# Hybrid encoder block: first weights in tiles of their own, the second unit's product ahead of the norm sum, and buffers placed at equal bytes modulo 512

## The chip, the cores and the metric

The kernel runs on one core of one Trainium2 chip. The metric is the device time of one execution in microseconds (us). Lower is better. A core has a matrix engine (PE; its weight loads are listed apart as PEld), a vector engine (DVE), a scalar engine (ACT), a general engine (POOL) and a queue engine (SP) that issues most transfers. Matrix products read two operands from the on-chip memory SBUF (a stationary one, loaded first, and a moving one, streamed past it) and write to PSUM, which has eight banks here, each holding one tile of 128x512 floats.

## The reference

One residual block over 512 frames of 1024 features:

```python
x = x + 0.5 * swiglu(rms_norm(x, ffn1_norm), ffn1_w1, ffn1_w3, ffn1_w2)   # D_FF = 2816
h = rms_norm(x, mix_norm); p = h @ w_in
y_a = rwkv7(token_shift(p_rwkv)) @ rwkv_proj      # 8 heads, delta-rule state
y_b = forgetting_attention(p_fox) @ fox_proj      # 8 heads
x = x + (sigmoid(g_a) * y_a + sigmoid(g_b) * y_b) @ w_out
x = x + 0.5 * swiglu(rms_norm(x, ffn2_norm), ffn2_w1, ffn2_w3, ffn2_w2)
out = rms_norm(x, final_norm)

def rms_norm(x, g): return x * rsqrt(mean(x * x) + 1e-6) * g
def swiglu(h, w1, w3, w2): return (silu(h @ w1) * (h @ w3)) @ w2
```

## The kernel before, in words

The activations are kept transposed: `xT` is eight tiles of 128 features by 512 frames. Every float operand of a large product is split into a high part in a reduced float format and a low part, the remainder (`xh`/`xl` for the scaled input, `whi`/`wlo` for weights, `hh`/`hl` for the hidden layer). `mm3` (line 124) makes each product out of three: high by high, high by low, low by high. One product of 128x128 weights with a 128x512 tile is one matmul instruction, so eight 128-feature slices give 24 instructions for one tile of output.

**Weights.** `load_raw` (line 105) brings 128x1024 floats (512 KB) into one of three `raw` buffers through SP's queue. `split_w` (line 111) casts them to `whi` on ACT and subtracts to `wlo` on DVE (on POOL where told so). There are two `whi` and two `wlo` buffers.

**The first FFN.** A unit `j` of the 22 hidden tiles takes two output tiles, `pa` (w1) and `pb` (w3), 24 instructions each. They are evacuated with the factor `rstd` of the norm: `fa = pa * rstd`, `fs = silu(fa)`, `fb = pb * rstd`, `fh = fb * fs`, and then split to `hh`, `hl`. The norm's factor is applied behind the product, so that the products need only `xT` times the gain. The first unit's products (named `f` in the trace) are run while the input is still arriving and being transposed (`xtp`, line 231). Then `Norm.finish` (line 189) adds up the squares, splits the sum, forms the sum over all features with two matmuls by a matrix of ones (`ssum`), and takes the root (`rln`, `rstd`) on ACT. After the 22 units come the down products `pd` (line 345): eight output tiles of 66 instructions, moving operand `hh` or `hl`. The second FFN is the same with other weights, its last output tile cut into two halves of 256 frames.

**The middle.** The mixer's input product (tiles `pk`, `pgt`, `pq`, `pv`), the chunked delta rule, attention, two projections (`ppj`, moving operands `yh`/`yl` and `ya`) and the output product (`pw`, moving operands `mh`/`ml`).

**PSUM.** Three pools: `pm` with two banks, `pr` with three, `pf` with three. `f0`, `f1`, every `pa`, `pd`, `pw`, `ppj` and `pgt` take a bank of `pm`; `pb`, `xtp` and `ssum` take one of `pr`.

**Order.** The code is recorded once. A scheduler then fixes each engine's order from its own estimate of times, within what the code allows; at run time each engine takes its instructions strictly in that order, each waiting for its own inputs and for its output buffer.

**Places in SBUF.** Tiles are laid one behind the other by pool in 32-byte steps. The following places are bytes within a partition, modulo 512, as the tile sizes give them; weights slices are 512 bytes apart and frame tiles 2048, so all slices of one buffer have the same remainder.

| buffers | before | changed |
|---|---|---|
| `raw`, `whi`, `wlo`, `xh`, `xl`, `acc`, `rstd`, temporaries | 288 | 288 |
| `hh`, `hl` (hidden layer of both FFNs), `xin` | 416 | 288 |
| mixer pool `sp`: `G`, `BK`, `RD`, `Tall`, and in their place later `ya`, `mh`, `ga` | 320 | 288 |
| `V4` (later `ml1`) | 320 | 288 |
| `qk`, `kb`, `klc`, `tr`, `vt`, and later `yh`, `yl` | 480 | 288 |
| most work tiles of the mixer's preparation (`t2`) | 416 | 224 |
| `xT` | 480 | 480 |
| `ident`; `center`, `bonesr`, `onesr` | 128; 384 | 128; 384 |

Of the kernel before, what the change touches and what calls it, by code (L numbers as in the profile page):

```python
# [36 lines left out]
PAR_Q, PAR_K, PAR_F = 66, 67, 68  # L37
PAR_N = 69

COL_W = 3 * DA  # L40
# [10 lines left out]
def kernel(  # L51
# [51 lines left out]

    def load_raw(aps, kt, n):
        raw = wp.tile([P, kt, n], F32, tag="raw", name="raw", bufs=3)
        for c0, src in aps:
            nc.sync.dma_start(raw[:, :, c0:c0 + src.shape[1]],
                              src.rearrange("(k p) c -> p k c", p=P))
        return raw

    def split_w(raw, kt, n, eng=None, own=None):
        if own is None:
            hi = wp.tile([P, kt, n], F32R, tag="whi", name="whi", bufs=2)
            lo = wp.tile([P, kt, n], F32R, tag="wlo", name="wlo", bufs=2)
        else:
            hi, lo = [xp.tile([P, kt, n], F32R, tag=f"x{i}{own}", name=f"own{i}{own}") for i in "hl"]
        act.copy(hi[:], raw[:])  # L117
        (eng or dve).tensor_tensor(lo[:], raw[:], hi[:].bitcast(F32), op=ALU.subtract)  # L118
        return hi, lo
# [14 lines left out]

    def exact(ps, mat, src):
        hi, lo = tmp("shi", dt=F32R), tmp("slo", dt=F32R)
        act.copy(hi[:], src)
        dve.tensor_tensor(lo[:], src, hi[:].bitcast(F32), op=ALU.subtract)
        pe.matmul(ps, mat[:], hi[:], start=True, stop=False)
        pe.matmul(ps, mat[:], lo[:], start=False, stop=True)  # L140

# [10 lines left out]
    class Norm:  # L152
# [35 lines left out]

        def finish(s):
            ps = bank("ssum", pr)  # L190
            dve.tensor_tensor(s.acc[:], s.acc[:], s.last[:], op=ALU.add)
# [4 lines left out]
            act.activation(s.rstd[:], ln[:], AF.Exp, scale=-0.5)  # L196

        def cols(s, ps, whi, wlo, m, holes=()):
# [15 lines left out]
    for _ in range(8):  # L214
        pe.matmul(warm[:, 0:P], ones[:], ones[:], start=True, stop=True)
    gtp = bank("gtp", pr)
# [3 lines left out]
    with tc.tile_pool(name="x0", bufs=1) as x0:  # L220
        xin = [x0.tile([P, NB, D // 4], F32, name=f"xin{g}") for g in range(4)]
        first = []
        for g in range(4):
            nc.sync.dma_start(xin[g][:], x[0, :, g * 256:(g + 1) * 256].rearrange("(b p) c -> p b c", p=P))
            for w, at in ((ffn1_w1, 0), (ffn1_w3, 1)):
                if g == at:
                    first.append(load_raw([(0, w[0][:, 0:P])], KD, P))
        for c in range(KD):
            ps = bank("xtp", pr)
            for b in range(NB):  # L230
                pe.transpose(ps[:, b * P:(b + 1) * P], xin[c // 2][:, b, (c % 2) * P:(c % 2 + 1) * P], ident[:])
            cx = act.copy(xT[c][:], ps[:])
            nrm.scale(c, act if (85 >> c) & 1 else dve)
            for i, at in enumerate((0, 2)):
                if c == at:
                    first[i] = (bank(f"f{i}"), split_w(first[i], KD, P, (dve, pool)[i]))
# [71 lines left out]
    def ffn(nrm, w1, w3, w2, nxt, during=(), first=None, final=None):  # L308
        with tc.tile_pool(name="hp", bufs=1) as hp:
            hh, hl = [], []  # L310
            for j in range(KF):
                c0 = j * P
                if j == 0 and first:
# [11 lines left out]
                a = tmp("fa")  # L325
                dve.tensor_tensor(a[:], pa[:], nrm.rstd[:], op=ALU.mult)  # L326
                sa = tmp("fs")
                act.activation(sa[:], a[:], AF.Silu)
                b = tmp("fb")
                dve.tensor_tensor(b[:], pb[:], nrm.rstd[:], op=ALU.mult)  # L330
                h = tmp("fh")
                dve.tensor_tensor(h[:], b[:], sa[:], op=ALU.mult)
                hi = hp.tile([P, T], F32R, name=f"hh{j}")
                lo = hp.tile([P, T], F32R, name=f"hl{j}")
                split(hi[:], lo[:], h[:], "dve")
                hh.append(hi)
                hl.append(lo)
            cuts = ((0, 8), (8, 8), (16, 6))
# [40 lines left out]
    with ExitStack() as mx:  # L379
# [21 lines left out]
        dve.tensor_scalar(omu[:], par[:, PAR_MU:PAR_W0], -1.0, 1.0, op0=ALU.mult, op1=ALU.add)  # L401

        def shifted(o, src, rows, mu):
# [58 lines left out]

        PC = rp.tile([P, NP, NC], F32, name="PC")
        Ld = dp.tile([P, C, C], F32, name="Ld")
# [222 lines left out]
        for b in range(NB):  # L687
            o = vtp.tile([P, T], F32, name=f"vt{b}", tag=f"vt{b}")
            act.activation(o[:], vps[b][:], AF.Copy, scale=rc[:, b:b + 1])
# [98 lines left out]
        for p in range(NP):  # L788
# [5 lines left out]
            for q in range(2):  # L794
# [229 lines left out]
```

## Time and profile before

| what | value |
|---|---|
| median of three runs | 1213.7 us (1209.55 to 1213.95) |
| span of the profiled execution | 1210.2 us |
| the profiled execution's own time beside the span | not listed on the page; the median run is 3.5 us above the span |
| PE busy | 1184.5 us, 98% of the span |
| DVE, ACT, POOL busy | 55%, 38%, 8% |
| transfers | 122.54 MB, mean 101 GB/s |

The page gives busy time by engine; busy matmul time includes overlap of one matmul with the next, so the distance from start to start tells more than the duration of one. A row of the timeline reads: start in us, duration in us, engine, line, operation, output<-inputs, and in brackets how long the engine had been idle and what released it. A row of the windows view gives, for one stretch of time, each engine's busy time with the number of instructions, then the granted clock of PE (1.00 is full), the transfers' share and GB/s.

### The profile page before, as it was taken

To read this page: it belongs to the slowest core of one execution; us is meant where nothing else is said; L and a number is where in the kernel's file an instruction comes from. 1 tells how busy PE (TensorE), PEld (TensorE's weight loads), DVE (VectorE), ACT (ScalarE), POOL (GpSimd) and SP (SyncE) were. 2 spreads that over 40 slices of the span, in tenths; PEclk is the share of its full clock that TensorE was granted. 3 is DMA by queue.
4 is the path that set the end of the run, shared out by engine and by line. 5 is a ranking of instruction groups with operands and counts; after the bars stand their busy time and mean duration, and the time that the engine had idled before them with its cause. 6 is when DMAs were issued, how large, how long until landed. Compare 5 with 4: busy or idle time off the path is not lost.

```text
span 1210.2 us, 15874 instructions
## 1 busy us (share of the span) xinstructions
PE 1184.5 (98%) x6334; PEld 955.1 (79%) x6334; DVE 665.2 (55%) x993; ACT 458.1 (38%) x739; POOL 100.5 (8%) x144
## 2 busy tenths in 40 slices
PE   8999999999999999999999999999999999999997
PEld 6788888888887788887667777678888888888887
DVE  7454555443443688776766666865554445443232
ACT  5222222222222854445867655523322222222221
POOL 4100000001111111321000011111000000000110
PEclk9999999999999999999999999999999999999999
DMA  6233233333334234345113235532333333323331
GB/s 186 73 95 105 87 105 88 104 95 108 107 111 106 76 104 124 109 135 131 36 36 102 63 97 163 178 106 87 103 102 92 100 104 88 104 80 96 96 96 70
DMA packets 208152, 122.54 MB, mean 101 GB/s; under 512 B 9902, under 2 KB 200430, under 8 KB 208078
## 3 DMA queue, kind: packets, MB, share of 16 engines
q1 hardware_dynamic: 202078, 108.67, 31.1%
q0 software_dynamic: 3760, 12.06, 3.2%
q8 instruction: 50, 0.82, 0.3%
q10 hardware_dynamic: 2240, 0.79, 0.3%
q14 instruction: 24, 0.20, 0.1%
HBM read 110.82 MB, written 10.68 MB: 100 GB/s over the span
## 4 chain that ended last, share of the span: by engine, by line
PE 93%; DVE 3%; ACT 1%; issue 0%; DMA 0%; DVEq 0%; POOL 0%; POOLq 0%
PE pd L127 7%; PE pd L125 7%; PE pd L126 7%; PE pa L125 7%; PE pa L126 7%; PE pa L127 6%; PE pb L127 6%; PE pb L126 6%; PE pb L125 6%; PE pgt L125 3%; PE pgt L127 2%; PE pgt L126 2%; PE pk L125 2%; PE pk L127 2%; PE pk L126 2%; PE pw L127 1%
## 5 line engine op out<-in xcount | busy, mean ns | idle before, releaser
L117 ACT CAST whi<-raw 128x1024 fp32r<-128x1024 f32 (+3 forms) x199 | 198.2, 998 | 631.2 <-PE pa L126 180.7
L118 DVE TENSOR_TENSOR wlo<-raw,whi 128x1024 fp32r<-128x1024 f32 (+2 forms) x198 | 229.5, 1159 | 142.3 <-ACT whi L117 142.2
L125 PE MATMUL pa<-xh,whi 128*128 128x512 f32 x344 | 134.7, 392 | 2.6 <-DVE fa L326 2.6
L127 PE MATMUL pb<-xh,wlo 128*128 128x512 f32 x344 | 134.5, 391 | 0.9 <-DVE wlo L118 0.9
L126 PE MATMUL pa<-xl,whi 128*128 128x512 f32 x344 | 134.6, 391 | 0.0
L125 PE MATMUL pb<-xh,whi 128*128 128x512 f32 x344 | 134.5, 391 | 0.0
L126 PE MATMUL pb<-xl,whi 128*128 128x512 f32 x344 | 134.5, 391 | 0.0
L127 PE MATMUL pa<-xh,wlo 128*128 128x512 f32 x344 | 134.4, 391 | 0.0
L127 PE MATMUL pd<-hh,wlo 128*128 128x512 f32 x330 | 130.8, 396 | 0.0
L125 PE MATMUL pd<-hh,whi 128*128 128x512 f32 x330 | 130.3, 395 | 0.0
L126 PE MATMUL pd<-hl,whi 128*128 128x512 f32 x330 | 130.3, 395 | 0.0
L330 DVE TENSOR_TENSOR fb<-pb,rstd 128x512 f32<-128x512 f32 x43 | 29.7, 691 | 137.5 <-PE pb L127 137.5
L125 PEld LDWEIGHTS pa<-xh,whi 128*128 128x128 f32 x344 | 64.9, 189 | 16.7 <-DVE fa L326 3.1
L127 PEld LDWEIGHTS pb<-xh,wlo 128*128 128x128 f32 x344 | 65.0, 189 | 14.8 <-DVE wlo L118 1.3
L127 PEld LDWEIGHTS pa<-xh,wlo 128*128 128x128 f32 x344 | 65.0, 189 | 13.6
L126 PEld LDWEIGHTS pa<-xl,whi 128*128 128x128 f32 x344 | 65.0, 189 | 13.5
L126 PEld LDWEIGHTS pb<-xl,whi 128*128 128x128 f32 x344 | 65.0, 189 | 13.5
L125 PEld LDWEIGHTS pb<-xh,whi 128*128 128x128 f32 x344 | 64.9, 189 | 13.5
L126 PEld LDWEIGHTS pd<-hl,whi 128*128 128x128 f32 x330 | 62.0, 188 | 14.9
L125 PEld LDWEIGHTS pd<-hh,whi 128*128 128x128 f32 x330 | 62.0, 188 | 14.6
L127 PEld LDWEIGHTS pd<-hh,wlo 128*128 128x128 f32 x330 | 62.0, 188 | 14.6
L326 DVE TENSOR_TENSOR fa<-pa,rstd 128x512 f32<-128x512 f32 x43 | 29.7, 692 | 73.6 <-PE pa L127 73.6
(395 smaller groups left out, 1968.0 us busy)
## 6 DMA issues: line engine op xcount, KB each, us to landing
raw<-in_ffn_w_dram SPq DMA_DIRECT2D x118, 512.0 KB
raw<-in_w_in_dram SPq DMA_DIRECT2D x40, 512.0 KB
raw<-in_ffn_w_dram SPq DMA_DIRECT2D x15, 384.0 KB
raw<-in_w_out_dram SPq DMA_DIRECT2D x8, 512.0 KB
gsave<-gs SPq DMA_DIRECT2D x9, 256.0 KB
xin<-in_x_dram SPq DMA_DIRECT2D x4, 512.0 KB
xsave<-xT POOLq DMA_DIRECT2D x8, 256.0 KB, 2.3
G<-gsave POOLq DMA_DIRECT2D x8, 256.0 KB, 3.8
```

The lines of the kernel that those rows point to most:

```text
L117: act.copy(hi[:], raw[:])
L118: (eng or dve).tensor_tensor(lo[:], raw[:], hi[:].bitcast(F32), op=ALU.subtract)
L125: pe.matmul(ps, whi, xhi, start=first, stop=False)
L126: pe.matmul(ps, whi, xlo, start=False, stop=False)
L127: return pe.matmul(ps, wlo, xhi, start=False, stop=last)
L326: dve.tensor_tensor(a[:], pa[:], nrm.rstd[:], op=ALU.mult)
L330: dve.tensor_tensor(b[:], pb[:], nrm.rstd[:], op=ALU.mult)
```

## The change

In words:

- The first unit's weights get raw tiles and split tiles of their own, in the pool `x0` that holds the input while it arrives (`wraw`, `first`). The three `raw`, two `whi` and two `wlo` buffers are then free for the second unit from the start.
- The second unit's `pa` takes a bank of the pool `pf`, where it took one of `pm`.
- `Norm.finish` is cut into `gather` (last addition and split), `sums` (the two matmuls) and `root` (logarithm and exponential). In the first FFN `gather` stands ahead of the second unit, and `sums` is to be issued only after the last matmul of the second unit's `pa`. The evacuation of a unit waits in a list until `rstd` is there.
- The matrix `ones` loses its own buffer (a temporary for the start, then the same bits read out of `onesr`); `tiny` and the `mx` tiles are widened to 32 floats, `PC` and the `vt` tiles are allocated earlier, and 48 floats are added behind `vt`. This moves the buffers as in the table above.

No arithmetic instruction is added or taken away.

```diff
-    ones = cp.tile([P, P], F32, name="ones")
-    dve.memset(ones[:], 1.0)
+    ones_ = tmp("ones", (P, P))
+    dve.memset(ones_[:], 1.0)
     onesr = cp.tile([P, P], F32R, name="onesr")
-    dve.tensor_copy(onesr[:], ones[:])
+    dve.tensor_copy(onesr[:], ones_[:])
+    ones = onesr[:].bitcast(F32)
...
+        elif isinstance(own, int):
+            hi, lo = [xp.tile([P, kt, n], F32R, tag=f"x{i}{own}", name=f"own{i}{own}") for i in "hl"]
         else:
-            hi, lo = [xp.tile([P, kt, n], F32R, tag=f"x{i}{own}", name=f"own{i}{own}") for i in "hl"]
+            hi, lo = own
...
-    def exact(ps, mat, src):
+    def halved(src):
         hi, lo = tmp("shi", dt=F32R), tmp("slo", dt=F32R)
         act.copy(hi[:], src)
         dve.tensor_tensor(lo[:], src, hi[:].bitcast(F32), op=ALU.subtract)
-        pe.matmul(ps, mat[:], hi[:], start=True, stop=False)
-        pe.matmul(ps, mat[:], lo[:], start=False, stop=True)
+        return hi, lo
+
+    def summed(ps, mat, parts):
+        for i, part in enumerate(parts):
+            pe.matmul(ps, mat[:], part[:], start=i == 0, stop=i == 1)
...
-        def finish(s):
-            ps = bank("ssum", pr)
+        def gather(s):
             dve.tensor_tensor(s.acc[:], s.acc[:], s.last[:], op=ALU.add)
-            exact(ps[:], onesr, s.acc[:])
+            s.parts = halved(s.acc[:])
+
+        def sums(s):
+            s.ps = bank("ssum", pr)
+            summed(s.ps[:], onesr, s.parts)
+
+        def root(s):
             ln = tmp("rln")
-            ln_act(ln[:], ps[:], bias=epsr[:, 0:1], scale=1.0 / D)
+            ln_act(ln[:], s.ps[:], bias=epsr[:, 0:1], scale=1.0 / D)
...
         xin = [x0.tile([P, NB, D // 4], F32, name=f"xin{g}") for g in range(4)]
+        own = [[x0.tile([P, KD, P], F32R, name=f"first{i}{w}") for i in "hl"] for w in range(2)]
+        wraw = [x0.tile([P, KD, P], F32, name=f"wraw{w}") for w in range(2)]
...
-                    pa = bank("pa")
+                    pa = bank("pa", pf if early else pm)
                     pb = bank("pb", pr)
                     for ps, w in ((pa, w1), (pb, w3)):
-                        nrm.cols(ps[:], *load_w([(0, w[0][:, c0:c0 + P])], KD, P), P)
+                        mms = nrm.cols(ps[:], *load_w([(0, w[0][:, c0:c0 + P])], KD, P), P)
+                        if early and w is w1:
+                            with tc.issue_after(mms[-1].ins):
+                                nrm.sums()
+                            nrm.root()
+                            evacuate()
                 if j == 0:
-                    nrm.finish()
+                    nrm.gather()
+                    if not first:
+                        nrm.sums()
+                        nrm.root()
...
-        tiny = rp.tile([P, 2], F32, name="tiny")
+        tiny = rp.tile([P, PAD], F32, name="tiny")
...
+        vts = [vtp.tile([P, T], F32, name=f"vt{b}", tag=f"vt{b}") for b in range(NB)]
+        vtp.tile([P, 48], F32, name="vtpad", tag="vtpad")
...
-            mx_ = [tp.tile([P, 2 * NB], F32, tag=f"mx{q}", name=f"mx{q}", bufs=2) for q in range(2)]
+            mx_ = [tp.tile([P, PAD], F32, tag=f"mx{q}", name=f"mx{q}", bufs=2) for q in range(2)]
```

How the instructions move is seen at three places. The first is PE's order at the end of the first unit's products (`f`). Before, the sum over features follows at once:

```order
L127 MATMUL f0_156<-xh7_274,wlo_158 128x512
L125 MATMUL f1_187<-xh7_274,whi_188 128x512
L126 MATMUL f1_187<-xl7_275,whi_188 128x512
L127 MATMUL f1_187<-xh7_274,wlo_189 128x512
L139 MATMUL ssum_317<-shi_319,onesr_87 128x512
L125 MATMUL pb_343<-xh0_152,whi_376 128x512
```

Now the second unit's `pa` follows:

```order
L132 MATMUL f1_189<-xh7_274,firstl1_141 128x512
L130 MATMUL pa_322<-xh0_156,whi_326 128x512
L131 MATMUL pa_322<-xl0_157,whi_326 128x512
L132 MATMUL pa_322<-xh0_156,wlo_327 128x512
L130 MATMUL pa_322<-xh1_172,whi_326 128x512
L131 MATMUL pa_322<-xl1_173,whi_326 128x512
```

All 24 matmuls of that `pa` stand ahead of the first `ssum`; the second `ssum` stands behind eleven of `pb`'s 24 matmuls, where it stood behind 23.

The second place is ACT's order around the squares (`sq`) and the second unit's weight casts (`whi`). Before:

```order
L178 ACTIVATE sq_295<-xT4_112 128x512
L178 ACTIVATE sq_298<-xT5_113 128x512
L178 ACTIVATE sq_301<-xT6_114 128x512
L178 ACTIVATE sq_304<-xT7_115 128x512
L117 CAST whi_346<-raw_344 128x1024
L117 CAST whi_376<-raw_374 128x1024
L137 CAST shi_319<-acc_284 128x512
L130 ACT_TABLE_LOAD
```

Now both casts and the table load stand among the squares; DVE's subtractions (`wlo`) stand likewise between its additions of the squares:

```order
L189 ACTIVATE sq_295<-xT4_112 128x512
L122 CAST whi_326<-raw_324 128x1024
L135 ACT_TABLE_LOAD
L122 CAST whi_376<-raw_374 128x1024
L189 ACTIVATE sq_298<-xT5_113 128x512
L189 ACTIVATE sq_301<-xT6_114 128x512
L189 ACTIVATE sq_304<-xT7_115 128x512
L142 CAST shi_318<-acc_284 128x512
```

The third place is SP's queue behind the input. Before, the loads of the second unit (`raw_344`, `raw_374`) and of the third (`raw_418`) stand apart, with small parameter rows between them:

```order
L224 DMA xin3_137<-in_x_dram 128x4x256
L107 DMA raw_344<-in_ffn1_w1_dram 128x8x128
L277 DMA rows_308<-in_mix_norm_dram 8x128
L277 DMA rows_308<-in_ffn2_norm_dram 8x128
L277 DMA rows_308<-in_shift_mu_dram 12x128
```

Now the three loads follow the input directly and the rows come behind them:

```order
L247 DMA xin3_137<-in_x_dram 128x4x256
L110 DMA raw_324<-in_ffn1_w1_dram 128x8x128
L110 DMA raw_374<-in_ffn1_w3_dram 128x8x128
L110 DMA raw_418<-in_ffn1_w1_dram 128x8x128
L300 DMA rows_308<-in_mix_norm_dram 8x128
```

Behind the third unit, every engine's order is as before.

More of the change, by code (lines that the diff above doesn't have):

```diff
@@ L101, with load_raw @@
     sel = cp.tile([P, 8], F32, name="sel")
-    def load_raw(aps, kt, n):
-        raw = wp.tile([P, kt, n], F32, tag="raw", name="raw", bufs=3)
+    def load_raw(aps, kt, n, raw=None):
+        if raw is None:
+            raw = wp.tile([P, kt, n], F32, tag="raw", name="raw", bufs=3)
         for c0, src in aps:
@@ L214 @@
     for _ in range(8):
-        pe.matmul(warm[:, 0:P], ones[:], ones[:], start=True, stop=True)
+        pe.matmul(warm[:, 0:P], ones_[:], ones_[:], start=True, stop=True)
     gtp = bank("gtp", pr)
@@ L235 @@
                 if c == at:
-                    first[i] = (bank(f"f{i}"), split_w(first[i], KD, P, (dve, pool)[i]))
+                    first[i] = (bank(f"f{i}"), split_w(first[i], KD, P, (dve, pool)[i], own[i]))
             for i, at in enumerate((0, 2)):
@@ L309, in ffn, with evacuate @@
         with tc.tile_pool(name="hp", bufs=1) as hp:
-            hh, hl = [], []
+            hh, hl, done = [], [], []
+            def evacuate():
+                while done:
+                    j, pa, pb = done.pop(0)
+                    a = tmp("fa")
+                    dve.tensor_tensor(a[:], pa[:], nrm.rstd[:], op=ALU.mult)
+                    sa = tmp("fs")
+                    act.activation(sa[:], a[:], AF.Silu)
+                    b = tmp("fb")
+                    dve.tensor_tensor(b[:], pb[:], nrm.rstd[:], op=ALU.mult)
+                    h = tmp("fh")
+                    dve.tensor_tensor(h[:], b[:], sa[:], op=ALU.mult)
+                    hi = hp.tile([P, T], F32R, name=f"hh{j}")
+                    lo = hp.tile([P, T], F32R, name=f"hl{j}")
+                    split(hi[:], lo[:], h[:], "dve")
+                    hh.append(hi)
+                    hl.append(lo)
             for j in range(KF):
                 c0 = j * P
+                early = j == 1 and first
                 if j == 0 and first:
@@ L324, in ffn @@
                         during[j]()
[L325 to L337, printed above, removed]
+                done.append((j, pa, pb))
+                if nrm.rstd is not None:
+                    evacuate()
             cuts = ((0, 8), (8, 8), (16, 6))
```

13 lines of the change are left out of this document (10 added, 3 removed).

## The prediction

> **What bounds the kernel now.** I read the page first, then the chain, then the start in windows and instruction by instruction.
>
> ```profile
> span 1210.2 us, 15874 instructions
> PE 1184.5 (98%) x6334; PEld 955.1 (79%) x6334; DVE 665.2 (55%) x993; ACT 458.1 (38%) x739; POOL 100.5 (8%) x144
> PE 93%; DVE 3%; ACT 1%; issue 0%; DMA 0%; DVEq 0%; POOL 0%; POOLq 0%
> ```
>
> PE is busy 98% of the span and holds 93% of the chain that ends last; transfers hold none of it. So time can only come from two things: places where PE stands still or runs at a lower clock, and the distance from one matmul's start to the next. The windows of the start show the first (PE, PEld, DVE, ACT, POOL busy, then the granted clock):
>
> ```profile
> core 0: us, PE busy (x) PEld busy (x) DVE busy (x) ACT busy (x) POOL busy (x), PEclk, DMA share, GB/s
> 24.41:27.82 3.41, 1.29 (x4) 0.79 (x5) 3.41 (x3) 2.43 (x3) 3.32 (x3) 1.00 0.13 37
> 27.82:31.24 3.42, 3.42 (x10) 2.65 (x8) 0.63 (x1) 0.00 (x0) 2.94 (x15) 0.50 0.87 257
> 34.65:38.06 3.41, 0.81 (x4) 0.68 (x5) 2.52 (x3) 3.35 (x5) 0.00 (x0) 1.00 0.05 16
> 38.06:41.48 3.42, 3.42 (x10) 2.68 (x9) 1.81 (x3) 0.35 (x1) 0.00 (x0) 0.50 0.47 138
> ```
>
> Twice PE works only 1.29 and 0.81 us of 3.41, and each time the next 3.4 us run at a clock of 0.50. The timeline names the waits:
>
> ```profile
> 23.53 0.39 PE L127 MATMUL f<-xh,wlo 128*128 128x512 f32 x1
> 25.61 0.50 PE L139 MATMUL ssum<-shi,onesr 128*128 128x512 f32 x1 [1.70 <-ACT shi L137]
> 27.49 0.53 PE L127 MATMUL pb<-xh,wlo 128*128 128x512 f32 x1 [0.91 <-DVE wlo L118]
> 34.21 0.40 PE L127 MATMUL pb<-xh,wlo 128*128 128x512 f32 x1
> 37.25 0.50 PE L125 MATMUL pa<-xh,whi 128*128 128x512 f32 x1 [2.64 <-DVE fa L326]
> 49.87 0.39 PE L125 MATMUL pb<-xh,whi 128*128 128x512 f32 x1
> ```
>
> PE waits for the norm sum's operand, then for the second unit's `wlo`, and after `pb` for `fa`, which empties the bank of `pm` that `pa` needs. The engines behind these waits:
>
> ```profile
> 17.56 1.15 ACT L178 ACTIVATE sq<-xT 128x512 f32<-128x512 f32 x2
> 18.01 2.32 DVE L168 SCALAR_TENSOR_TENSOR xl<-xT,par,xh 128x512 fp32r<-128x512 f32 x2
> 23.05 1.99 ACT L117 CAST whi<-raw 128x1024 fp32r<-128x1024 f32 x2 [1.38 <-PE f L126]
> 23.43 0.91 DVE L191 TENSOR_TENSOR acc<-acc,sq 128x512 f32<-128x512 f32 x1
> 24.26 3.17 DVE L118 TENSOR_TENSOR wlo<-raw,whi 128x1024 fp32r<-128x1024 f32 x2
> 25.58 1.28 ACT L130 ACT_TABLE_LOAD   x1
> 35.13 0.68 ACT L132 ACTIVATE rln<-ssum,epsr 128x512 f32<-128x512 f32 x1
> 35.84 0.63 ACT L196 ACTIVATE rstd<-rln 128x512 f32<-128x512 f32 x1
> 36.50 0.69 DVE L326 TENSOR_TENSOR fa<-f,rstd 128x512 f32<-128x512 f32 x1
> ```
>
> The casts at 23.05 were released by PE: the second unit's weights had to wait until the first unit gave up its `whi` buffers.
>
> The second thing shows in PE's starts, in the up products, the down products and a projection, and for `pw` in a window of matmuls alone:
>
> ```profile
> 130.11 0.39 PE L125 MATMUL pb<-xh,whi 128*128 128x512 f32 x1
> ...
> 131.47 0.39 PE L125 MATMUL pa<-xh,whi 128*128 128x512 f32 x1
> ```
>
> ```profile
> 299.97 0.40 PE L125 MATMUL pd<-hh,whi 128*128 128x512 f32 x1
> ...
> 302.30 0.40 PE L126 MATMUL pd<-hl,whi 128*128 128x512 f32 x1
> ```
>
> ```profile
> 780.63 0.40 PE L125 MATMUL ppj<-ya,whi 128*128 128x512 f32 x1
> ...
> 782.97 0.40 PE L126 MATMUL ppj<-ya,whi 128*128 128x512 f32 x1
> ```
>
> ```profile
> 804.00:834.00 30.00, 30.00 (x130) 1.00 0.37 108
> ```
>
> Up: 6 steps in 1.36 us, 226.7 ns. Down: 10 steps in 2.33 us, 233 ns. `ppj`: 10 steps in 2.34 us, 234 ns. `pw`: 130 in 30 us, less one cut at the edges, 233 ns. All are the same instruction at full clock with no wait. What differs is the place: `xh` and `whi` both lie at 288 modulo 512, while `hh` is at 416, `ya` and `mh` at 320, `yh` at 480.
>
> **The first part of the change: the start.** Had PE gone on after the `f` at 23.53 at 226.7 ns, it would have had 74 matmuls to issue before the `pb` that stands at 49.87 (24 `pa` and 24 `pb` of unit two, two `ssum`, 24 `pa` of unit three): 23.76 + 74 x 0.2267 = 40.5. So 9.3 us are lost there: the idle stretches are 25.61 - 23.76 = 1.9, about 1.1 ahead of 27.49 and 37.25 - 34.44 = 2.8, together 5.7, and the half clock takes the other 3.6 (ten matmuls in a window where fifteen would fit, twice). The new order is worth 9.3 us if no wait takes their place. Each one in turn, with durations from the rows above:
>
> - *Loads.* Seven loads of 512 KB now stand in one queue. The transfers' view of the first 60 us, in 40 slices of 1.5 us:
>
> ```profile
> GB/s 0 139 354 277 352 304 334 345 303 285 121 5 102 282 62 3 0 2 225 210 251 12 0 0 0 209 141 0 0 0 0 0 210 139 5 62 287 11 0 80
> ```
>
>   The first nine slices carry 3.6 MB, that is seven loads by 13.5 us; two more at some 0.3 MB/us are there by 17.1. The input keeps its place ahead of them, and the parameter rows come later for nobody: they are used from the eleventh unit on.
> - *Casts.* ACT ends the square ahead of them at about 18.1; `whi` takes 1.0, the table load 1.28, the second `whi` 1.0, three squares 0.6 each: 23.3. DVE ends `xl` at 20.3, adds one square (0.9), makes `wlo` (1.6) by 22.8. `pa` wants that `wlo` at its third matmul, 24.2. Slack 1.4 us.
> - *Norm sum.* DVE goes on with an addition, the second `wlo` and three additions, at the same durations (0.9, 1.6): 28.0. The cast `shi` takes 0.6 like a square of the same size, so 28.6. PE gets to `ssum` at 23.76 + 24 x 0.2267 = 29.2. Slack 0.6 us.
> - *Root and bank.* The second `ssum` starts at 29.4 + 11 x 0.2267 = 31.9 and ends near 32.3. From `rln`'s start to the `pa` behind `fa` took 37.25 - 35.13 = 2.1 us: 34.5. PE ends `pb` at 35.1. Slack 0.6 us. ACT's third weight cast no longer delays `rln`, since its buffer is free at 29.2. Behind a late `fa` stand DVE's `fb` and `fh` and the next `wlo`, which PE wants only at 41.
>
> The second unit's bank in `pf` is idle there (its users are the warm-up and the mixer), and the cut of `finish` adds no instruction: nothing for both. I take 9.3, the upper bound. The lower one: one slack fails by the 1.1 us of the shortest wait above, and one half-clock window returns (1.8): 6.4.
>
> By the Trainium skill's page "TensorE: Matmul & The Clock Gate" (Part 1, the HAM clock gate) PE falls to half clock after an idle window of about 3.4 us. Here windows with 1.29 and 0.81 us of work did it, so the measurement decides; by the rule the gaps would not be the cause, only the 5.7 us of idle time would go, and the sum would be 3.6 us smaller.
>
> **The second part: the places.** After it `hh`, `hl`, `ya`, `mh`, `ml`, `yh`, `yl` lie at 288 like the weights. The trace has one pair of places at one remainder (226.7) and three different pairs at different ones (233 to 234). Matmuls concerned:
>
> ```profile
> L125 PE MATMUL pd<-hh,whi 128*128 128x512 f32 x330 | 130.3, 395 | 0.0
> L125 PE MATMUL pw<-mh,whi 128*128 128x512 f32 x64 | 25.3, 398 | 0.5 <-ACT whi L117 0.5
> L125 PE MATMUL ppj<-ya,whi 128*128 128x512 f32 x32 | 13.0, 416 | 2.2 <-ACT whi L117 1.6 <-ACT ya L143 0.7
> L125 PE MATMUL ppj<-yh,whi 128*128 128x512 f32 x32 | 13.1, 411 | 0.2 <-DVE gs L633 0.2
> ```
>
> Each row is one of three like it: 3 x (330 + 64 + 32 + 32) = 1374, times 6.5 ns = 8.9 us. PE sets the pace in all of them: `pd` has no idle time, and the up products feed the same loads and casts faster today. In the projection DVE comes nearest:
>
> ```profile
> 771.00:797.00 26.00, 25.74 (x110) 20.42 (x111) 19.73 (x30) 12.00 (x20) 0.00 (x0) 1.00 0.49 149
> ```
>
> 19.7 of 26 us are DVE's, so 3% less on PE is still not its bound. The bounds: below nothing, no row lets me expect a loss, since the pair at equal remainders is the fastest; zero, if the remainder is not the cause. Above, 8.9 plus half of 6.5 ns for the 132 half-width products of the last tile (0.4). I take 8.9, because the rows of `pd`, `ppj` and `pw` agree with it, at three different remainders. `tiny`, `mx`, `PC`, `vt` and `ones` change places only: no instruction, nothing.
>
> **The sum.** 9.3 + 8.9 = 18.2 us: the span goes from 1210.2 to 1192.0. The median of the runs shown is 3.5 us above that span; taken from the median, 1213.7 - 18.2 = **1195.5 us**.
>
> **Rivals.**
>
> *The remainder is not what slows `pd`.* The slow tiles also lie higher in SBUF. For it: nothing in this trace has moved a tile. Against: `hh` begins directly behind the temporaries and is slow from its first matmul. It gives 1213.7 - 9.3 = 1204.4. The Trainium skill's page "SBUF — State Buffer" (Who interferes with whom) says that only the port pair shared by DVE and GpSimd contends and that PE never waits on anyone; by that rule places would be worth nothing and this rival would come true. The 226.7 against 233 ns at full clock and with no wait do not agree with it.
>
> *A new wait at the start.* The norm sum has the smallest margin with the longest string of DVE work ahead of it. If POOL's casts stretch that work by 2 us more, `ssum` holds PE for 1.4 us, and if that window falls to half clock another 1.8 go: 9.3 - 3.2 = 6.1, so 1213.7 - 6.1 - 8.9 = 1198.7.
>
> *The gain is given back.* The middle (412 to 710 us) is a braid of PE, DVE and ACT, and coming earlier may change nothing there; but a shift of all engines alike cannot be lost, so this needs both parts to fail: no new order at the start because a load is late, and equal places worth nothing. Time 1210 to 1214.
>
> *Slower.* The preparation's work tiles go from 416 to 224 and attention's tiles from 480 to 288, beside constants that stay. If DVE minds remainders as PE seems to, it is in these stages that it would pay:
>
> ```profile
> 412.00:560.00 148.00, 147.48 (x856) 120.43 (x857) 117.84 (x189) 74.79 (x106) 31.12 (x57) 0.99 0.41 113
> 600.00:710.00 110.00, 106.67 (x1094) 81.11 (x1094) 72.14 (x167) 79.13 (x205) 1.97 (x4) 0.98 0.21 61
> ```
>
> 190 us of DVE work; it turns the result when these grow by more than 18.2 / 190 = 9.6%, and at 15% the time is 1213.7 - 18.2 + 28.5 = 1224. Against it:
>
> ```profile
> L144 DVE TENSOR_TENSOR hl<-fh,hh 128x512 fp32r<-128x512 f32 x20 | 13.8, 692 | 0.7
> L332 DVE TENSOR_TENSOR fh<-fb,fs 128x512 f32<-128x512 f32 x20 | 13.8, 692 | 2.0
> ```
>
> The first mixes 288 and 416, the second is all 288, and both take 692 ns.
>
> **How the numbers follow.** Both parts as worked out: 0.75, 1195.5, own range 1191 to 1199 (below: the last tile and the spread of the runs shown, whose lowest is 4 us under the median). Places worth nothing: 0.10. A new wait: 0.08. Given back: 0.04. Slower: 0.03. The range 1190 to 1204.5 holds the first three. A change within 0.5% (6.1 us) cannot be told from none here: faster 0.93, same 0.04, slower 0.03.
>
> **What would show it.** Right: the three waits at 25.61, 27.49 and 37.25 are gone, no window between 24 and 42 us has a clock of 0.50, the third unit's `pb` begins near 40.5; `pd`, `pw` and `ppj` start every 226.7 ns, so that 100 us of `pd` hold 441 matmuls, not 429. Wrong: `pd` still at 233 ns (places); a wait for `shi` or `fa` above 1 us (the margins); longer DVE rows between 412 and 710 us (the slower case).

## The result and the profile after

Four runs of the changed kernel have a median of 1194.6 us (1191.7 to 1195.2), four of the kernel before beside them 1212.2; the ratio is 0.9851 (95% interval 0.9832 to 0.987). The forecast was 1195.5. The profiled execution's span is 1193.5 us against 1210.2, that is 16.8 us less before rounding, and all differences below are made between these two. The head of the page after:

```profile
span 1193.5 us, 15868 instructions
PE 1172.4 (98%) x6334; PEld 953.9 (80%) x6334; DVE 663.8 (56%) x993; ACT 458.3 (38%) x739; POOL 101.1 (8%) x144
```

PE does the same 6334 matmuls and is as full as before. Its busy time fell by 12.1 us and its idle time by 4.7, so most of the gain is time that matmuls took. The start in windows (PE, PEld, DVE, ACT, POOL busy with counts, then the granted clock):

```profile
core 0: us, PE busy (x) PEld busy (x) DVE busy (x) ACT busy (x) POOL busy (x), PEclk, DMA share, GB/s
4.97:8.38 3.41, 1.17 (x9) 0.91 (x9) 0.70 (x2) 1.61 (x3) 0.00 (x0) 1.00 1.01 303
8.38:11.79 3.41, 3.38 (x12) 3.14 (x13) 3.22 (x6) 3.01 (x5) 0.00 (x0) 0.50 1.11 334
24.41:27.82 3.41, 3.41 (x17) 2.83 (x16) 2.51 (x4) 0.62 (x1) 3.28 (x4) 1.00 0.89 258
34.65:38.06 3.41, 3.41 (x17) 2.83 (x16) 2.76 (x6) 2.93 (x4) 0.88 (x1) 1.00 0.06 19
38.06:41.48 3.42, 3.42 (x17) 2.83 (x16) 3.38 (x6) 0.65 (x2) 0.00 (x0) 1.00 0.41 119
```

The two gaps and the two windows of 0.50 behind them are gone: in every window from 24 to 41 us PE is at work throughout, at a clock of 1.00. A new window of 0.50 stands at 8.38, behind one with 1.17 us of work. PE's timeline at the four places that the forecast named, and its waits in the first 60 us (engine, line, what was waited for, then total, times and longest in us):

```profile
23.88 0.39 PE L132 MATMUL f<-xh,firstl 128*128 128x512 f32 x1
24.11 0.39 PE L130 MATMUL pa<-xh,whi 128*128 128x512 f32 x1
...
29.55 0.39 PE L148 MATMUL ssum<-shi,onesr 128*128 128x512 f32 x1
...
32.29 0.39 PE L148 MATMUL ssum<-slo,onesr 128*128 128x512 f32 x1
...
40.93 0.39 PE L130 MATMUL pb<-xh,whi 128*128 128x512 f32 x1
```

```profile
PE xtp L254 <- DMA xin<-in_x_dram: 2.3, 1, 2.3
PE warm L236 <- DVE ones L84: 1.1, 1, 1.1
PE f L131 <- DVE xl L179: 0.2, 1, 0.2
```

No row has a wait behind 23.88, and the third unit's `pb` begins at 40.93 instead of 49.87. The places show in a count of matmuls: the same 100 us of the first down product before and after, and 100 us of the second one (its transposes counted too).

```profile
262.00:362.00 100.00, 100.00 (x430) 80.48 (x429) 40.63 (x42) 22.81 (x26) 13.07 (x11) 1.00 0.36 109
1076.00:1176.00 100.00, 100.00 (x444) 80.95 (x444) 31.92 (x37) 24.17 (x29) 8.72 (x5) 1.00 0.31 90
```

```profile
262.00:362.00 100.00, 100.00 (x443) 82.81 (x442) 41.17 (x41) 23.63 (x27) 15.56 (x13) 1.00 0.38 112
1062.00:1162.00 100.00, 100.00 (x454) 82.77 (x453) 33.27 (x37) 25.17 (x30) 8.84 (x5) 1.00 0.32 94
```

430 against 443 (the ones cut at the edges count). Where the 16.8 us went, by the starts of the first or last matmul of each stage in the timelines:

| point | before, us | after, us | gained since the row above |
|---|---|---|---|
| last `f` of the first unit | 23.53 | 23.88 | -0.35 |
| first `pd`, first feed-forward part | 262.17 | 253.24 | 9.29 |
| last `pd` | 385.14 | 372.69 | 3.51 |
| first `ppj` (mixer and attention between) | 733.11 | 720.73 | -0.07 |
| first `pw` | 788.34 | 775.18 | 0.78 |
| last `pw` | 834.53 | 820.22 | 1.15 |
| first `pd`, second part (up products between) | 1074.65 | 1060.30 | 0.04 |
| last `pd` of the full-width tiles | 1184.96 | 1168.05 | 2.56 |
| end of the span | 1210.2 | 1193.5 | -0.1 |

### The profile page after: what moved, and what is told of

Same layout as the page of the kernel before. It is cut to its first block, busy times and chain, and to the rows that moved or that the text cites. A ratio compares the mean times of both kernels' runs of the same rounds, so it can differ in the third digit from the quotient of the medians.

```text
span 1193.5 us, 15868 instructions
## 1 busy us (share of the span) xinstructions
PE 1172.4 (98%) x6334; PEld 953.9 (80%) x6334; DVE 663.8 (56%) x993; ACT 458.3 (38%) x739; POOL 101.1 (8%) x144
## 4 chain that ended last, share of the span: by engine, by line
PE 94%; DVE 3%; ACT 1%; DMA 1%; issue 0%; SPq 0%; POOL 0%; DVEq 0%; POOLq 0%
PE pd L131 7%; PE pd L130 7%; PE pd L132 7%; PE pa L132 7%; PE pa L130 7%; PE pb L132 7%; PE pb L130 7%; PE pa L131 7%; PE pb L131 7%; PE pgt L130 3%; PE pgt L132 2%; PE pgt L131 2%; PE pk L130 2%; PE pk L132 2%; PE pk L131 2%; PE pw L132 1%
## 5 line engine op out<-in xcount | busy, mean ns | idle before, releaser
L122 ACT CAST whi<-raw 128x1024 fp32r<-128x1024 f32 (+2 forms) x197 | 196.4, 998 | 605.8 <-PE pa L131 176.0
```

## The experiments

### Each part alone

The first run keeps the new order at the start and puts every tile back where it lay; the second does the opposite. The first, against the change:

```diff
-        tiny = rp.tile([P, PAD], F32, name="tiny")
+        tiny = rp.tile([P, 2], F32, name="tiny")
...
-        vtp.tile([P, 48], F32, name="vtpad", tag="vtpad")
...
+    ones = cp.tile([P, P], F32, name="ones")
```

> The changed kernel with its new start, but every buffer at the place it had before (hidden layer at 416, mixer pool at 320, attention tiles at 480, weights and scaled input at 288 modulo 512). Theory (two independent gains): the start is worth about 9 us, pd, pw and ppj stay at 233 to 234 ns from start to start, so the span is about 1201 us (ratio to the kernel before 0.9925). Rival (the start gives everything, the 226.7 ns come with it): span 1193.5, pd at 226.7 ns. Rival (the places give everything): span about 1210.

The second, against the kernel before: the same lines the other way round, and nothing at the start.

> The kernel before with nothing but the places of the change. Theory: pd, pw and ppj start every 226.7 to 228 ns, the three waits and the two half-clock windows of the start stay, the span falls by about 7.8 us to 1202.4 (ratio 0.9936), and this and the start-only kernel's gain add up to the whole change's 16.8 us within 1 us. Rival (gains overlap or need each other): the sum of the two is less than 15 us.

Measured: 1203.2 us for the start alone (ratio 0.9936, 0.9918 to 0.9954; span 1201.8) and 1203.6 us for the places alone (0.9937, 0.9921 to 0.9954; span 1202.0). By their spans they save 8.4 and 8.2 us, together 16.6 of 16.8, so the parts add up. The same 100 us of the first down product, start alone and then places alone:

```profile
262.00:362.00 100.00, 100.00 (x430) 80.43 (x430) 37.72 (x38) 22.56 (x26) 13.08 (x11) 1.00 0.37 110
```

```profile
262.00:362.00 100.00, 100.00 (x443) 82.81 (x442) 40.64 (x42) 22.82 (x26) 13.07 (x11) 1.00 0.38 112
```

The first gains 9.28 us between the last `f` and the first `pd`, loses 0.75 ahead of it, and is as long as before, to 0.1 us, in everything behind. The second gains 3.51, 0.78, 1.21 and 2.56 us in `pd`, `ppj`, `pw` and the second `pd`, and 0.02 up to the first `pd`.

### The two halves of the start

The new order has two supports: tiles of their own for the first unit's weights, and the idle bank with the norm sum in steps behind it. The first run here takes away the tiles:

```diff
-                    first.append(load_raw([(0, w[0][:, 0:P])], KD, P, wraw[at]))
+                    first.append(load_raw([(0, w[0][:, 0:P])], KD, P))
...
-                    first[i] = (bank(f"f{i}"), split_w(first[i], KD, P, (dve, pool)[i], own[i]))
+                    first[i] = (bank(f"f{i}"), split_w(first[i], KD, P, (dve, pool)[i]))
```

> The change with the first unit's weights in the shared buffers again (raw, halves and remainders); the idle bank, the early sum and the places stay. By the prediction's first step the second unit's half part can't be cast until PE has read the last f of the first unit: it starts near 23 us, and the remainder part is done near 25.5 instead of 23.0, against the 24.2 at which PE wants it. PE then stands 1.3 us or more, and if that costs a half-clock window another 1.7: span 1194.8 to 1197, a ratio of 0.986 to 0.990. Rival (the idle bank alone removes the wait, the tiles of its own do nothing): span 1193.5, and no wait of PE between 23 and 30 us.

The second keeps the tiles and takes away the bank and the steps:

```diff
-                early = j == 1 and first
+                early = False
...
-                    if not first:
-                        nrm.sums()
-                        nrm.root()
+                    nrm.sums()
+                    nrm.root()
```

> The change with the second unit's first product in the shared banks again and the sum of squares and the root at their old place, straight behind the first unit; the weights' own tiles and the places stay. By the prediction the second product of unit two still waits for the first unit's banks, and these for the root: PE's wait on fa stays near 2.7 us and brings a half-clock window, so that about 2.7 us and 1.7 to 3.4 us of the change's gain are gone: span 1197.5 to 1200. Rival (the own tiles carry the start's gain): span 1193.5 to 1195.

Without the tiles: 1195.4 us (0.9874, 0.9857 to 0.989), span 1195.5, within the expected range. PE's waits and two windows there (the granted clock changes only at steps of 3.41 us, whose place differs from run to run; these steps are called its grid, and the windows are cut along it):

```profile
PE pa L132 <- DVE wlo L123: 1.0, 1, 1.0
...
PE pa L130 <- ACT whi L122: 0.2, 1, 0.2
```

```profile
24.15:27.57 3.42, 2.14 (x8) 1.16 (x7) 2.81 (x3) 3.39 (x4) 3.29 (x4) 1.00 0.00 0
27.57:30.98 3.41, 3.41 (x16) 2.82 (x15) 1.76 (x2) 0.05 (x1) 3.14 (x11) 1.00 0.75 215
```

`whi` is late by little and `wlo` by 1.0, and 2.14 us of work in a window were enough to keep the clock. The bank alone gains 7.45 us between the last `f` and the first `pd`.

Without the bank, both theories missed: 1206.4 us (0.9959, 0.9946 to 0.9973), span 1204.8, which is 11.3 us over the change where 4 to 6.5 were expected. PE's timeline and DVE's:

```profile
28.00 0.79 PE L148 MATMUL ssum<-shi,onesr 128*128 128x512 f32 x1 [3.73 <-ACT shi L142]
...
39.68 0.51 PE L130 MATMUL pa<-xh,whi 128*128 128x512 f32 x1 [2.93 <-DVE fa L339]
```

```profile
21.31 1.21 DVE L123 TENSOR_TENSOR wlo<-raw,whi 128x1024 fp32r<-128x1024 f32 x1
...
23.05 1.21 DVE L123 TENSOR_TENSOR wlo<-raw,whi 128x1024 fp32r<-128x1024 f32 x1
24.18 2.10 DVE L191 TENSOR_TENSOR acc<-acc,sq 128x512 f32<-128x512 f32 x2
26.39 0.91 DVE L201 TENSOR_TENSOR acc<-acc,sq 128x512 f32<-128x512 f32 x1
```

The expectation had kept the wait on `fa` and forgotten the one on `shi`. Casts that can start early are queued on DVE ahead of the additions of the squares, so the norm sum comes 2 us later than in the kernel before (the wait grew from 1.70 to 3.73), and PE meets it at once, since no product of the second unit stands ahead of it. The two waits are 6.7 us. The rest is clock, as the windows of this run show, with columns as above:

```profile
23.21:26.63 3.42, 1.06 (x5) 0.56 (x3) 3.21 (x4) 0.00 (x0) 2.98 (x3) 1.00 0.67 189
26.63:30.04 3.41, 2.04 (x5) 1.65 (x6) 1.36 (x2) 1.90 (x2) 3.11 (x10) 0.50 0.42 126
30.04:33.45 3.41, 3.41 (x10) 2.64 (x9) 0.00 (x0) 0.00 (x0) 3.06 (x8) 0.50 0.00 0
36.87:40.28 3.41, 0.60 (x3) 0.51 (x4) 2.42 (x3) 3.33 (x4) 0.00 (x0) 1.00 0.01 4
40.28:43.69 3.41, 3.41 (x10) 2.63 (x9) 1.81 (x3) 0.01 (x1) 0.00 (x0) 0.50 0.50 149
```

PE ran at half speed from 28.00 to 33.45 and for 3.41 us from 40.28, and half of 8.9 us is 4.4; 6.7 + 4.4 = 11.1 of the 11.3. So the tiles alone make the start 2.1 us longer than it was before (240.75 us between the last `f` and the first `pd`, against 238.64), the bank alone 7.45 shorter, and both 9.29 shorter: the tiles pay only where PE has a product to do while the norm sum is made. A bank of the shared pool with the sum behind `pa` is no third case: `pa` would wait for a bank that only `fa` frees, and `fa` for the sum that comes behind `pa`.

### Are the gaps the cause of the half clock?

The kernel before with PE kept at work in its two gaps, and no wait removed:

```diff
+                    idle = bank("idle", pf)
+                    with tc.issue_after(lastmm[j].ins):
+                        for _ in range((7, 11)[j]):
+                            pe.matmul(idle[:], onesr[:], nrm.hi[0][:], start=True, stop=True)
```

> The kernel before, with seven extra matmuls of 512 columns on PE behind the last f and eleven behind the second unit's second product, into a bank that is otherwise not used. None of the waits is taken away; PE only isn't idle in them. If PE's idle stretches in 24 to 35 us are what brings the two half-clock windows at 27.82 and 38.06, the records show no granted clock of 0.50 between 24 and 42 us and the span is shorter by what the two windows cost, 3.0 to 3.6 us: 1206.6 to 1207.2 instead of 1210.2, a ratio near 0.997. Rival (the windows come from something else than idle stretches on PE, or an added matmul lengthens a wait as much as the window cost): both windows stay, and the span is 1210 to 1212.

The windows of this run at the places where the kernel before had its gaps and its half clock:

```profile
24.41:27.82 3.41, 3.23 (x13) 1.99 (x11) 3.31 (x4) 3.39 (x4) 3.31 (x4) 1.00 0.00 0
27.82:31.24 3.42, 2.58 (x11) 2.16 (x12) 1.40 (x2) 0.18 (x1) 3.11 (x11) 1.00 0.70 200
34.65:38.06 3.41, 3.33 (x14) 2.39 (x14) 2.54 (x4) 3.29 (x5) 0.19 (x1) 1.00 0.15 44
38.06:41.48 3.42, 3.42 (x16) 2.82 (x16) 1.79 (x3) 0.00 (x0) 0.00 (x0) 1.00 0.37 109
```

The half clock is gone from this stretch, and it is 3.15 us shorter between the last `f` and the first `pd`. The grid lies within 0.1 us of where it lay in the kernel before (27.90 against 27.82), so its place is not the reason. The gaps cause the half clock, and waits and clock can be had apart. The whole span says less: it is 1206.5, 3.7 us shorter, but 1.1 us were lost ahead of the last `f`, and 1.4 were won near 628 us, where this execution had no half-clock window and the one of before had. The medians give 0.9978 (0.9964 to 0.9991).

### What it is about the places

First, is it height in SBUF, or 288, or the difference between the two operands? The change with one pad that moves the weights to 416 (and with them `hh`, `hl`, `ya`, `mh`, `ml`), while `xh`, `xl` and `yh` stay at 288:

```diff
             s.rstd = xp.tile([P, T], F32, tag="rstd", name="rstd")
+            xp.tile([P, 32], F32, tag="xpad", name="xpad")
```

> The changed kernel with 128 bytes of padding behind the scaled input, so that weights, hidden layer and mixer pool lie at 416 while xh and xl stay at 288. Theory (what counts is the difference between the moving operand and the weights): pd (416 with 416), pw and ppj from ya stay at 226.7 ns; the up products and the mixer's input products (288 with 416), 3072 matmuls, go to 233 ns, the span to about 1212 us. Rival (the moving operand's own remainder of 288 is what is fast): the up products stay at 226.7, pd goes to 233, span about 1200 us.

Measured 1213.8 us, span 1212.1: all of the change's gain, lost by 128 bytes. A window of 100 us of up products and one of down products, and behind them the same window of up products in the change:

```profile
60.00:160.00 100.00, 100.00 (x432) 80.81 (x432) 48.72 (x65) 24.36 (x27) 0.00 (x0) 1.00 0.33 95
290.00:390.00 100.00, 100.00 (x442) 80.95 (x441) 41.33 (x47) 25.33 (x31) 15.56 (x14) 1.00 0.38 111
```

```profile
60.00:160.00 100.00, 100.00 (x443) 82.77 (x442) 50.47 (x68) 24.35 (x27) 0.00 (x0) 1.00 0.33 96
```

The up products fall from 443 to 432, and the down products, now with both operands at 416, stay at 442. The difference counts, not the place. Then a ladder: each hidden tile 32 bytes further than the one before, with the weights where they were.

```diff
+                    if j:
+                        hp.tile([P, 8], F32, name=f"pad{j}")
                     hi = hp.tile([P, T], F32R, name=f"hh{j}")
```

> The changed kernel with 32 bytes of padding ahead of each hidden tile from the second on, so that tile j lies at 288 + 32*j modulo 512; the weights stay at 288. Only the down products read these tiles. Theory (equal remainder modulo 512): tiles 0 and 16 start every 226.7 ns; tiles 1 (difference 32), 4 (128) and 6 (192) at 233 to 234, as the three pairs of the kernel before; the rest is unknown. Rival (a smaller modulus): tile 8, at a difference of 256, or tiles 4 and 12 are as fast as tile 0. Rival (height in the memory): no dependence on j modulo 16, tile 16 not faster than its neighbours.

Measured 1197.6 us in its only run, span 1195.8, and this in the same window of the first down product as above:

```profile
262.00:362.00 100.00, 100.00 (x431) 80.74 (x431) 38.70 (x40) 23.62 (x27) 13.45 (x12) 1.00 0.37 109
```

Against the change the first `pd` stage is 3.1 us longer and the second one 2.3. But tiles 0 and 16, whose difference is 0 modulo 512, took 230.8 and 231.4 ns, where the others took 228.6 to 234.4, and not 226.7. From tile 3 on, each tile took what the tile 8 places further took, to 0.1 ns, and 8 places are 256 bytes. Each tile has only three matmuls there, so its neighbours could matter. The sweep that was made for it holds one difference for a whole product of 24 matmuls, with the weights of the up products in tiles that can be moved by `d` bytes:

```diff
+                            d = 32 * (j - 2) + 256 * i if j < 10 else 32 * (j - 10) + 16 + 256 * i if j < 18 else 8 * (j - 18) + 4 * i
...
+                                t = hp.tile([P, KD * P + 128], F32R, tag=f"v{n}", name=f"v{n}", bufs=2)
+                                own.append(t[:, d // 4:d // 4 + KD * P].rearrange("p (k c) -> p k c", c=P))
```

> The weights of the up products of units 3 to 22 (half parts and remainder parts) lie in tiles that start d bytes behind the remainder (modulo 512) of the scaled input's tiles, with d constant inside a product: 0, 32, 64 ... 224 for the first product of units 3 to 10, and 256 more for the second product of the same units; 16 to 240 in steps of 32 and again 256 more for units 11 to 18; 0 to 28 in steps of 4 for units 19 to 22. All else as in the change. Theory as the prediction had it (only the same remainder modulo 512 is fast): 226.7 ns for d = 0 alone, 231 to 235 ns for every other d from 32 up, 256 among them. Theory after the ladder (modulo 256): d and d + 256 within 1 ns of each other, 226.7 ns for d = 0 and d = 256, 231 to 235 ns between. Rival (the history of tiles in the ladder and not the distance set its rate): all d alike, 226.7 or 233 ns. In the first two the span is some 900 matmuls by 5 to 6.5 ns longer than the change's 1193.5 us, 1198 to 1199.5; in the rival 1193.5 or 1199.5.

Measured 1199.9 us, span 1198.2. The starts of the products with d = 256 (first row; 22 matmuls up to `pa`), 128 and 384 (three rows from 81.62), 192 and 448 (three from 103.98):

```profile
35.73 0.39 PE L130 MATMUL pb<-xh,vh 128*128 128x512 f32 x1
...
40.71 0.39 PE L130 MATMUL pa<-xh,vh 128*128 128x512 f32 x1
...
81.62 0.39 PE L130 MATMUL pa<-xh,vh 128*128 128x512 f32 x1
...
87.21 0.40 PE L130 MATMUL pb<-xh,vh 128*128 128x512 f32 x1
...
92.78 0.40 PE L130 MATMUL pa<-xh,vh 128*128 128x512 f32 x1
...
103.98 0.40 PE L130 MATMUL pa<-xh,vh 128*128 128x512 f32 x1
...
109.49 0.39 PE L130 MATMUL pb<-xh,vh 128*128 128x512 f32 x1
...
114.98 0.40 PE L130 MATMUL pa<-xh,vh 128*128 128x512 f32 x1
```

(40.71 - 35.73) / 22 = 226.4 ns (226.7 inside the product); 5.59 and 5.57 us for 24, 232 to 233; 5.51 and 5.49, 229 to 230. From the starts of each product's matmuls behind the eighth:

| d modulo 256 | 0 | 16 | 32 | 48 | 64 | 80 | 96 | 112 | 128 | 144 | 160 | 176 | 192 | 208 | 224 | 240 |
|---|---|---|---|---|---|---|---|---|---|---|---|---|---|---|---|---|
| ns, below 256 | 226.7 | 233.2 | 233.5 | 233.4 | 233.5 | 232.0 | 234.3 | 233.3 | 232.4 | 233.4 | 233.3 | 230.0 | 228.9 | 232.1 | 233.2 | 228.5 |
| ns, 256 and above | 226.7 | 233.2 | 233.5 | 233.4 | 233.5 | 232.0 | 234.5 | 233.3 | 232.3 | 233.4 | 233.3 | 230.0 | 228.9 | 231.7 | 233.2 | 228.5 |

Each pair agrees to 0.4 ns: the period is 256 bytes, and of the multiples of 16 only 0 has the full rate. None of the 40 products is below 226.6 ns, so the change already has the best that places gave here. History counts too: the product with d = 0 behind the one with 496 took six matmuls, of 226 to 236 ns, before it ran at 226.7. That fits the ladder, where a tile has three matmuls at a time and none got there. Differences of 4 to 24 bytes gave 229.7 to 233.3. One of 28, whose first matmuls lie among `pd`'s, gave 226.7; whether the difference or that history did it stays open.

### A filler in the changed kernel

By the traces so far PE's half clock hangs on its work in stretches of 3.41 us, and the changed kernel still has three such stretches, near 8, 401 and 616 us. Two of them can be filled:

```diff
+            if c == 1:
+                with tc.issue_after(xt.ins):
+                    for _ in range(4):
+                        pe.matmul(warm[:, 0:P], ident[:], ident[:], start=True, stop=True)
...
+                for _ in range((1, (3, 4)[i])[p == NP - 1]):
+                    pe.matmul(ps[:], w_[0:96, p * P:(p + 1) * P], x_[0:96, :], start=True, stop=True)
```

> The change with two fillers on PE that take no wait away: four matmuls of 128 columns behind the first eight transposes, where PE stood 2.27 us for the input at 8.41, and the last two pz products issued three and four times over (the same numbers each time), where PE stood 0.80 and 0.78 us near 398 and 400. Theory from the traces so far: a half-clock stretch of 3.41 us follows a stretch of the same length in which PE worked less than 1.8 us, and none follows one with more than 2.1. The work in the stretches ahead of 8.38 and 400.91 rises from 1.17 and 1.79 us to more than 2.2, wherever the grid lies, so neither half-clock stretch comes; the pk products behind the second are some 1.6 us shorter (eight matmuls by 0.2 us), the last f comes at most 0.35 us earlier, because the input's transfers set that part. The stretch at 616 isn't touched and stays as the grid's place has it. Span 1191.5 to 1192 against 1193.5. Rival (the copies delay ACT, which reads pz, by as much, or the half clock comes from something else): span 1193.5 to 1194.5.

> The change itself, on the same chip as the filled one: a median of 1194.6 us, a span of 1193.5 if the grid of the clock lies as in its first profile, and up to 1.7 us more or less for each half-clock stretch that its place adds or leaves out.

Measured on one chip: filled 1193.2 us (0.9836, 0.9823 to 0.985), the change again 1192.4 (0.9833, 0.9819 to 0.9846). No difference. The profiled span of the filled one is 1190.7, and it has none of the three stretches, but its parts are not as expected, as PE's timeline near 400 us shows:

```profile
398.02 0.97 PE L498 MATMUL pz<-codes,uw 96*128 96x512 f32 x3 [0.79 <-ACT G L499]
398.83 1.08 PE L498 MATMUL pz<-codes,ux 96*128 96x512 f32 x4
400.69 0.50 PE L130 MATMUL pk<-xh,whi 128*128 128x512 f32 x1 [0.78 <-DVE u L534]
```

The copies did not fill the waits. They moved them: both are as long as before, and `pk` begins 0.8 us later than it would (400.69, in a run whose last `f` is 0.24 us earlier, against 400.13). Of the 1.6 us of half clock 0.8 are left as gain. The start gained 0.24, and 1.4 us came near 616 and 0.3 near 703, where nothing was edited; at 616 the grid lay elsewhere. At the start the work did not rise to the 2.2 us expected either:

```profile
5.66:9.07 3.41, 1.74 (x16) 1.58 (x15) 1.41 (x2) 2.48 (x4) 0.00 (x0) 1.00 1.07 309
```

No half clock followed all the same, so the rule of 1.8 us that this run was built on has an exception here, and it stays open why. Where the grid spares these places anyway, the copies can only cost, though no run measured that apart. The change stays the better kernel, being as fast and simpler.

## Why the prediction was right, point by point

- *The order at the start, 9.3 us.* Right: 9.29 from the last `f` to the first `pd`, 9.28 with the tiles' places undone. All three waits went and none came. Of the margins, the first `wlo` was done at 22.5, where 22.8 had been worked out. `shi` was done at 27.5 (it starts at 26.88 and takes 0.62), where 28.6 had been worked out, so the norm sum's slack was 2.0 us instead of 0.6: each `wlo` took 1.2 us where 1.6 had been taken.
- *The split into 5.7 us of waiting and 3.6 of clock.* Right within half a microsecond: filling the gaps without removing the waits gave 3.15 for the clock.
- *The clock gate.* The prediction set the row (1.29 and 0.81 us of work before a window of 0.50) over the rule of the Trainium skill's page "TensorE: Matmul & The Clock Gate" (Part 1, the HAM clock gate), which asks for an idle window. The kernel before with its gaps filled decides it: with 3.23 and 3.33 us of work in those windows no half clock follows. What the prediction left out is that the grid of these windows lies differently in each execution, so that the new kernel could get a half-clock window at 8.38 that the old one did not have. It also ends its last `f` 0.35 us later. That this comes from the half clock is not shown: the ladder has such a window at 8.85 and the filled run has none, and both end their last `f` at 23.64.
- *The places, 8.9 us from 1374 matmuls by 6.5 ns.* The mechanism was right (places alone: 8.2 us by the span, `pd`, `ppj` and `pw` at 226 to 228 ns); the term was 1 us too large. By its parts: the first `pd` 3.51 (3.43 by the count), `pw` 1.15 (1.25), the second `pd` 2.56 (3.0), `ppj` 0.78 (1.25), the last tile's half-width products nothing (up to 0.4 had been left open). The step that failed is "the rows agree", taken from three stretches and carried to all: the second `pd` went from 444 to 454 per 100 us, ten more and not thirteen. By the timelines, its undisturbed steps (from one matmul to the next, under 250 ns) went from 232.8 to 227.1 ns, which is 5.7 and not 6.5. In `ppj` only 171 of the 192 steps are undisturbed, they went from 233.2 to 228.1, and its waits took 0.1 us more (2.2 before, 2.3 now).
- *Modulo 512.* Too strict. The sweep shows 256; the places that the change gave to the operands of `pd`, `ppj` and `pw` meet both.
- *The remainder is not the cause (0.10).* Excluded by the 128-byte pad: the tiles hardly higher than before, and all the gain lost. It was the rival that the Trainium skill's page "SBUF — State Buffer" (Who interferes with whom) would have made true, with PE waiting on nobody; 226.7 and 233 ns at full clock and without a wait do not agree with it.
- *A new wait (0.08).* It did not come here; the run without the idle bank has it, at 3.7 us, which shows that the order, and not the tiles, holds it off.
- *Given back (0.04).* The stretch from the last `pd` to the first `ppj` is as long as before, to 0.07 us. A shift of all engines alike was neither lost nor added to.
- *Slower through DVE (0.03).* The same two stretches as in the prediction, 12.45 us earlier:

```profile
399.55:547.55 148.00, 147.42 (x856) 120.42 (x857) 117.87 (x189) 74.85 (x106) 31.27 (x57) 0.99 0.39 114
587.55:697.55 110.00, 106.67 (x1094) 81.21 (x1094) 72.22 (x167) 79.20 (x205) 1.92 (x4) 0.98 0.20 61
```

  DVE's 117.84 and 72.14 us became 117.87 and 72.22. So DVE shows no effect of the new places in these stretches.
- *The total.* 18.2 forecast, 16.8 by the spans: 1.0 too much for the places, 0.35 lost ahead of the last `f`. That the median came out within a microsecond is partly luck. In every listed run the time stands about 1.7 us above the span, but the sum was taken from a median 3.5 above the span of the profiled execution. These 1.8 us made up for the 1.4 forecast too much.

## What to carry to other kernels

Count matmuls per 100 us at full clock and without waits: where the same instruction stands at 430 in one stage and 443 in another, compare the byte addresses of its two operands, and give the moving one and the weights the same remainder modulo 256. Look for gaps that left PE under some 2 us of work in 3.4 here, because each can cost 1.7 us (half of 3.41) more than its own length, and take the wait away rather than fill it. When a buffer is freed earlier, look at what its earlier users now stand ahead of on their engine: here the freed weights were worth 1.8 us with a product to cover the norm sum and cost 2.1 without one.

## What the runs showed of the hardware that had not been expected

- *A grid of 3.41 us for PE's clock.* Half-clock stretches are 3.41 us long, or twice that, and lie on a grid of that step, whose place differs from one execution to the next. In the twelve traces, gone through window by window, every window at full clock with 1.82 us of work or less was followed by one at half clock (for instance 1.79 and then 0.50 at 400.91 in the change), except the one of 1.74 in the filled run. Between 1.84 and 2.09 both occur. Of the windows with more (for instance 2.14 and then 1.00 without the tiles) only one was followed by half clock, the last one with work in the start-only run, with 2.29. A window that is itself at half clock needs more: 2.04, 2.20 and 2.61 us in it were followed by another one, 3.06 and more were not. The Trainium skill's page "TensorE: Matmul & The Clock Gate" (Part 1, the HAM clock gate) has such a window, free-running and 3413 ns long, and the stretches here agree with both; its rule that the clock falls after an idle window does not agree, since a window with half its length at work was enough.
- *Runs of one kernel differ by it.* Five runs of the change on one chip have spans of 1190.3 to 1193.5 us, at a mean granted clock of 0.997 in the three short ones, 0.996 in the next and 0.994 in the longest. Each half-clock stretch full of work costs half its length, so two more are 3.4 us. A gain of 2 us can't be told from that by medians of a few runs; it can in a trace, stage by stage.
- *Operands 256 bytes apart.* 128x512 matmuls with a new weight load each take 226.7 ns when both operands have the same remainder modulo 256, and 228.5 to 234.5 when these differ by another multiple of 16, with patterns that repeat inside a product (225, 230, 235, 230 ns for a difference of 176). Why stays open.
